# Which products run beside the routing: 96 instead of 76 of 128 expert blocks, at a rate set by how many are left

## The chip, the core and the metric

The kernel runs on one core of one Trainium2 chip. The metric is the device time of one launch in microseconds; lower is better. Engines are named as the profile names them: PE is TensorE (matmuls), PEld its weight loads, DVE is VectorE, ACT is ScalarE, POOL is GpSimd, SP is SyncE, which here only issues DMAs.

## The reference

Two layers of a backbone, each an attention mixer followed by a PEER mixer over 16384 single-neuron experts; 128 prompt tokens and 512 sample tokens. The mixers are not touched. What matters is the second half of each layer:

```python
def peer(h, w_q, sub_keys, u, v):                 # x: tokens x 1024
    q = (x @ w_q).reshape(t, PEER_HEADS, 2, PEER_HALF)
    s = jnp.einsum('thcd,hcnd->thcn', q, sub_keys)
    s1, i1 = lax.top_k(s[:, :, 0], 16)
    s2, i2 = lax.top_k(s[:, :, 1], 16)
    ...                                            # 16 best of the 256 sums
    top_s, pos = lax.top_k(cand, 16)
    idx = jnp.take_along_axis(cidx, pos, axis=-1)
    g = jax.nn.softmax(top_s, axis=-1)
        a = jnp.einsum('td,thkd->thk', xb, u[ib])  # first product
        w = gb * jax.nn.gelu(a)
        return jnp.einsum('thk,thkd->td', w, v[ib])# second product
```

Each token picks 8 x 16 = 128 experts, and their rows of `u` and `v` (1024 floats each) make its output.

## The kernel before

The work is written as Python generators. Each `yield` gives a cost; `weave` runs a main generator and advances side tasks by that cost times their `rate`. What is emitted this way is then ordered on each engine by the scheduler of the framework, and each engine takes its instructions strictly in that order.

For the PEER mixer, 384 of the 512 sample tokens (three tiles of 128) are done densely: all 16384 experts, in 128 blocks of 128 experts, with a gate matrix that is zero where an expert was not picked. The other sample tile and the prompt are done by gathering expert rows with indirect DMAs (`gather_tile`, 256 gathers of 128 rows of 4 KB a tile). Each layer has three stages:

- **Mixer** of the sample, with the prompt's work and gathers beside it.
- **Routing** (`route`, called W in the code): the queries (`peer_q`), the choice of 16 (`pairs`), and then `gate_build` for each of three tiles, which turns indices into dense gate rows on DVE, ACT and PE and writes them to DRAM (`Gd`). A tile has 32 gate steps, each of 4 tokens, 8 small matmuls (L1403, L1404), two evictions (`gst`, L1407) and a `yield 2.2`; three tiles make 96 steps. Beside it runs `dense_pre`: for each block number in `PRE` it loads 512 KB of `ut`, splits it into `uhi` (ACT, L1422) and `ulo` (DVE, L1423), makes the first product for 384 tokens in 24 matmuls (L1434), applies the activation (ACT, tile `gpre`, L1436) and writes 192 KB to DRAM (`Ad`, L1443). What of it is not done when `route` ends is emitted in one piece (`t.drain()`).
- **Dense stage** (`dense`): for each of 128 blocks it loads `v` (512 KB), and either `pre` back from `Ad` (192 KB, blocks in `PRE`) or makes the first product on the spot (`gad`, with its own load of `ut`, for the others); then it multiplies by the gate (`W`, `Whi`, `Wlo`) and adds the second product in 18 matmuls of 512 columns (L1457). The gathers of rows and, in layer 0, the prompt's next mixer run beside it, at rates worked out from the dense stage's total cost.

`PRE` is a rule on the block number: three of every four blocks for the first `Q3` groups of four, two of four for the rest. The rate of `dense_pre` is `AR` = 0.3 up to the end of `peer_q`, `AP_` = 1.75 up to the gate steps, and `AB` = 1.0 in them; a block costs 4.0. The gathers' rate in the dense stage is

```python
total = 4.0 * (256 - len(PRE))
need = 256 * (l + 1)
gath.rate = (need - self.slots) * 3.1 / total * DM
```

so that it follows the dense stage's cost.

Of the kernel before, what the change touches and what calls it, by code (L numbers as in the profile page):

```python
# [28 lines left out]
ND = 384  # L29
NTG = ND // 32  # L30

Q3 = 12
PRE = [i for i in range(128) if i % 4 < (3 if i // 4 < Q3 else 2)]
GBUFS = 8
PTB = 2
# [26 lines left out]
PDR = 0.7  # L62
GA = 0.7
GB = 0.5
AB = 1.0
AR = 0.3
DM = 1.05

# [170 lines left out]
def weave(main, *tasks):  # L239

    tot = 0
    while not main.done:
        cost = main.step()
        tot += cost or 0
        for t in tasks:
            t.advance(cost or 0.0)


class K:
# [1188 lines left out]
    def dense_pre(self, l, Ad):  # L1438
        h = self.ss.h
        for n, i in enumerate(PRE):  # L1440
            ga = self.ph.tile([128, ND], F32, tag="ga", name="gpre", bufs=2)
            self.a_block(l, i, h, n % 8 >= QV, ga)
            self.nc.scalar.dma_start(Ad[n], ga)  # L1443
            yield 4.0

    def dense(self, l, st, h, Gd, Ad, gate):
# [151 lines left out]
    def route(self, l, Gd):  # L1598
        ss = self.ss
        self.ld("iota2", self.nc.scalar, self.ph)  # L1600
        m, gs = self.mg[l]
        ss.h = self.ada(ss, gs[:, 1, :, 1], m[:, 24:32, 1])
        self.flags.add(f"h{l}")
        yield 8.0
        yield from self.peer_q(l, ss)
        self.gath.rate, self.pre.rate = GP, AP_
        yield from self.pairs(ss, 3)
        self.flags.add(f"s{l}")
        yield from self.pairs(ss, 0)
        self.gath.rate, self.pre.rate = GB, AB  # L1610
        n = ND // 128
        for i in range(n):
            build = Task(self, self.gate_build(ss, i, Gd))
            nxt = Task(self, self.pairs(ss, i + 1) if i + 1 < n else iter(()), PRATE)
            build.ctx = nxt.ctx = self.ph, self.wk, self.wb
            while not build.done:
                yield build.step() or 0.0
                nxt.advance(2.2)
            while not nxt.done:
                yield nxt.step() or 0.0  # L1620
# [7 lines left out]
    def run(self, stop=99):  # L1628
# [7 lines left out]
        gath = Task(self, self.gathers(), GRATE)  # L1636
        for l in range(2):
            with self.psum(f"M{l}", mm=2, S=2, tr=1, acc=1):
                sample = Task(self, self.mixer(l, ss))
                if l == 0:  # L1640
                    ma, mp = ExitStack(), ExitStack()
                    pool = ma.enter_context(tc.tile_pool(name="mod1", bufs=1, reuse_waits="tile"))
                    ahead = Task(self, self.mod_strips(1), M1R)
                    ahead.ctx = (pool, pool, 6)
                    pool = mp.enter_context(tc.tile_pool(name="mod0", bufs=1, side="right", reuse_waits="tile"))
                    mod = Task(self, self.mod(0, ("acc", "tr", "acc"), "mw"), 2.0)
                    mod.ctx = (pool, pool, 6)
                    self.constants()
                    old = self.ph, self.wk
                    for st in (ss, sp):  # L1650
                        for _ in range(MS):
                            mod.step()
                        self.ph = self.wk = pool
                        r = self.rstd_x(st)
                        st.r0 = self.cst.tile([128, st.nt], F32, tag="r0" + st.name, name="r0" + st.name, bufs=1)
                        nc.vector.tensor_copy(st.r0, r)
                        self.ph, self.wk = old
                    for _ in range(9 - 2 * MS):
                        mod.step()
                    self.ph = self.wk = pool  # L1660
                    self.decays()
                    self.ld("lam", nc.scalar, pool)
                    self.lam()
                    self.ph, self.wk = old
                    while not mod.done:
                        mod.advance(sample.step())
                    mp.close()
                gath.rate = GRATE if l == 0 else GRATE1
                gath.credit = 0.0
                if l == 0:  # L1670
                    weave(sample, prompt, ahead, gath)
                    ahead.drain()
                    ma.close()
                else:
                    weave(sample, prompt, gath)
                while f"p{l}" not in self.flags:
                    prompt.step()
            gath.rate = GA
            prompt.rate = 0.5
            gath.credit = prompt.credit = 0.0  # L1680
            Gd = self.dram.tile([NTG, 128, 128, 32], F32, name=f"Gd{l}")
            Ad = self.dram.tile([len(PRE), 128, ND], F32, name=f"Ad{l}")
            with self.psum(f"W{l}", mm=W_MM, gb=W_GB), self.sbuf(f"W{l}"):
                ctx = (self.ph, self.wk, 3)
                route = Task(self, self.route(l, Gd))
                pre = Task(self, self.late(f"h{l}", self.dense_pre(l, Ad)), AR)
                self.pre, self.gath = pre, gath
                side = [gath, pre]
                for t in [route] + side[1:]:
                    t.ctx = ctx  # L1690
                weave(route, *side, prompt)
                for t in side[1:]:
                    t.drain()
            with self.psum(f"D{l}", **{f"d{t}{hf}": 1 for t in range(3) for hf in range(2)}, mm=1, pm=1), self.sbuf(f"D{l}"):
                dense = Task(self, self.dense(l, ss, ss.h, Gd, Ad, self.mg[l][0][:, 40:48, 1]))
                dense.ctx = (self.ph, self.wk, 3)
                gath.alias = prompt.alias = "pm"
                self.flags.add(f"d{l}")
                total = 4.0 * (256 - len(PRE))
                gath.credit = prompt.credit = 0.0  # L1700
                prompt.rate = PDR
                need = 256 * (l + 1)
                gath.rate = (need - self.slots) * 3.1 / total * DM
                weave(dense, gath, prompt)
                while f"so{l}" not in self.flags:
                    gath.step()
                while l == 0 and "p1" not in self.flags:
                    prompt.step()
                for t in (gath, prompt):
                    if l:  # L1710
                        t.drain()
                gath.alias = prompt.alias = None
            self.dump(f"xs{l}", ss)
# [39 lines left out]
```

## Time and profile before

| | |
|---|---|
| time, median of 3 runs | 4050.77 us (4027.24 to 4058.07) |
| time of the profiled execution | 4050.72 us |
| its span, first to last instruction | 4048.9 us |
| PE busy / PE weight loads busy | 3653.0 us / 3060.2 us |
| DVE / ACT / POOL busy | 3180.2 us / 1620.7 us / 1621.2 us |
| moved by DMA | 1134.86 MB, mean 280 GB/s |
| gate steps to first dense block, layer 0 / 1 | 1008.3 to 1308.6 us / 2935.3 to 3266.6 us |
| dense stage (first to last `Whi`), layer 0 / 1 | 1308.6 to 2183.2 us / 3266.6 to 4026.2 us |

A busy time is the union of an engine's instructions. Matmuls overlap in the pipeline, so a PE that is busy all the time need not be full; the distance from the start of one matmul to the start of the next tells more. The DMA share is the mean busy share of the 16 DMA engines.

### The profile page before, as it was taken

How to read it: one execution, taken by the hardware profiler on the slowest of the kernel's cores; microseconds unless marked ns; L12 is line 12 of the kernel's file. 1: busy time of each engine (PE TensorE's matmuls, PEld its weight loads, DVE VectorE, ACT ScalarE, POOL GpSimd, SP SyncE). 2: the span in 40 equal slices, each digit the busy share in tenths (PEclk: the TensorE clock that was granted, in tenths of full speed). 3: DMA queues.
4: the chain of work that ended last, by engine and by line, in shares of the span. 5: the costliest groups of instructions: out<-in, count | busy, mean ns of one | idle time of the engine just before them, and what ended most of it. 6: DMA issues, size and time to landing. Idle time of an engine off the chain costs nothing.

```text
span 4048.9 us, 57028 instructions
## 1 busy us (share of the span) xinstructions
PE 3653.0 (90%) x19986; PEld 3060.2 (76%) x19986; DVE 3180.2 (79%) x6370; ACT 1620.7 (40%) x2971; POOL 1621.2 (40%) x1138
## 2 busy tenths in 40 slices
PE   7888889889997999999998898988976999999998
PEld 3675556778886877888886676777875888888887
DVE  3238668999997767778897898899997667777777
ACT  3222223334776433433333333333476634333333
POOL 1004445320554234443464676532075233444342
PEclk9999989999998999999999999999997999999999
DMA  8556778775798889899896777777577889999886
GB/s 320 179 176 235 276 281 281 252 233 181 277 363 323 308 294 358 301 338 347 303 351 250 241 244 231 257 257 232 188 266 274 331 301 333 345 337 324 301 309 213
DMA packets 441087, 1134.86 MB, mean 280 GB/s; under 512 B 40640, under 2 KB 191360, under 8 KB 434528
## 3 DMA queue, kind: packets, MB, share of 16 engines
q0 software_dynamic: 147968, 537.36, 37.7%
q1 hardware_dynamic: 251408, 506.28, 36.3%
q10 hardware_dynamic: 41424, 87.57, 5.8%
q8 instruction: 157, 2.57, 0.2%
q14 instruction: 130, 1.06, 0.1%
HBM read 1045.08 MB, written 85.98 MB: 279 GB/s over the span
## 4 chain that ended last, share of the span: by engine, by line
PE 48%; DVE 16%; DMA 8%; issue 8%; ACT 5%; POOL 2%; ACTq 0%; DVEq 0%; POOLq 0%; SPq 0%
PE d L1457 21%; PE mm L1434 14%; PE mm L478 5%; DMA u<-ut 3%; DVE acc L1340 3%; DVE row L1336 2%; DMA row<-u,xi 2%; PE pm L482 2%; DVE ulo L1423 2%; ACT gst L1407 2%; POOL row L1323 1%; DMA Gd<-gst 1%; ACT uhi L1422 1%; PE S L708 1%; DMA Ad<-gpre 1%
## 5 line engine op out<-in xcount | busy, mean ns | idle before, releaser
L1323 POOL DMA_INDIRECT row<-v,xi x512 | 832.3, 1626 | 1114.1 <-DVE acc L1340 773.6
L1323 POOL DMA_INDIRECT row<-u,xi x512 | 681.3, 1331 | 789.0 <-DVE row L1336 585.2
L1434 PE MATMUL mm<-hhi,uhi 128*128 128x384 f32 x2048 | 709.6, 346 | 46.9 <-ACT uhi L1422 43.2
L1434 PE MATMUL mm<-hhi,ulo 128*128 128x384 f32 x2048 | 707.2, 346 | 49.3 <-DVE ulo L1423 49.1
L1434 PE MATMUL mm<-hlo,uhi 128*128 128x384 f32 x2048 | 702.6, 343 | 2.2 <-DVE hlo L452 1.6
L1336 DVE SCALAR_TENSOR_TENSOR row<-hn,row 128x1024 f32<-128x1024 f32 x512 | 630.0, 1257 | 47.4 <-DMA row<-u,xi 39.8
L1340 DVE SCALAR_TENSOR_TENSOR acc<-row,gw,acc 128x1024 f32<-128x1024 f32 x508 | 650.6, 1281 | 4.2 <-DMA row<-v,xi 1.6
L1457 PE MATMUL d<-vlo,Whi 128*128 128x512 f32 x1536 | 482.1, 394 | 5.6 <-DVE vlo L1498 5.6
L1457 PE MATMUL d<-vhi,Wlo 128*128 128x512 f32 x1536 | 479.0, 393 | 0.0
L1422 ACT CAST uhi<-u 128x1024 fp32r<-128x1024 f32 x256 | 268.8, 1050 | 491.8 <-PE mm L1434 226.8
L1423 DVE TENSOR_TENSOR ulo<-u,uhi 128x1024 fp32r<-128x1024 f32 x256 | 313.5, 1225 | 185.0 <-ACT uhi L1422 183.7
L1457 PE MATMUL d<-vhi,Whi 128*128 128x512 f32 x1536 | 437.3, 397 | 16.9 <-ACT vhi L1497 13.2
L1434 PEld LDWEIGHTS mm<-hhi,uhi 128*128 128x128 f32 x2048 | 396.5, 194 | 65.1 <-ACT uhi L1422 54.4
L1434 PEld LDWEIGHTS mm<-hhi,ulo 128*128 128x128 f32 x2048 | 395.3, 193 | 66.0 <-DVE ulo L1423 62.7
L1434 PEld LDWEIGHTS mm<-hlo,uhi 128*128 128x128 f32 x2048 | 395.2, 193 | 8.7 <-DVE hlo L452 2.0
L1457 PEld LDWEIGHTS d<-vhi,Whi 128*128 128x128 f32 x1536 | 288.1, 190 | 74.9 <-ACT vhi L1497 17.3
L1457 PEld LDWEIGHTS d<-vhi,Wlo 128*128 128x128 f32 x1536 | 288.0, 188 | 61.4 <-issue 0.2
L1457 PEld LDWEIGHTS d<-vlo,Whi 128*128 128x128 f32 x1536 | 286.4, 189 | 62.8 <-DVE vlo L1498 8.0
L1498 DVE TENSOR_TENSOR vlo<-v,vhi 128x1024 fp32r<-128x1024 f32 x256 | 312.2, 1221 | 14.2 <-ACT vhi L1497 13.9
L1505 ACT CAST Whi<-W 128x384 fp32r<-128x384 f32 x256 | 131.2, 513 | 433.1 <-PE d L1457 337.1
L1497 ACT CAST vhi<-v 128x1024 fp32r<-128x1024 f32 x256 | 268.5, 1051 | 53.3 <-DMA v<-v 41.9
L478 PE MATMUL mm<-hhi,whi 128*128 128x512 f32 x624 | 255.4, 410 | 31.5 <-DVE rvs L594 12.6
(470 smaller groups left out, 5776.4 us busy)
## 6 DMA issues: line engine op xcount, KB each, us to landing
u<-ut SPq DMA_DIRECT2D x256, 512.0 KB, 5.3
v<-v SPq DMA_DIRECT2D x256, 512.0 KB, 6.2
Gd<-gst ACTq DMA_DIRECT2D x48, 1024.0 KB, 8.7
G<-Gd SPq DMA_DIRECT2D x64, 768.0 KB, 8.8
w<-win SPq DMA_DIRECT2D x80, 512.0 KB, 4.7
w<-wq SPq DMA_DIRECT2D x64, 512.0 KB, 5.2
Ad<-gpre ACTq DMA_DIRECT2D x152, 192.0 KB, 4.5
pre<-Ad SPq DMA_DIRECT2D x152, 192.0 KB, 6.0
```

What stands on the lines that cost most here:

```text
L478: nc.tensor.matmul(ps[:, :st.T], wp[a][:, k], h[b][:, k], start=(n == 0), stop=(n == 23))
L482: nc.tensor.matmul(ps[:, :st.T], w32[:, k], h[:, k], start=(k == 0), stop=(k == 7))
L1323: nc.gpsimd.indirect_dma_start(out=r, out_offset=None, in_=self.A[f"{'uv'[n // 128]}{l}"], in_offset=bass.IndirectOffsetOnAxis(ap=xi[:, s: ...
L1336: nc.vector.scalar_tensor_tensor(r, hn, 1.0, r, op0=ALU.mult, op1=ALU.mult, accum_out=a[:, s:s + 1])
L1340: nc.vector.scalar_tensor_tensor(acc, r, w[:, s:s + 1], acc, op0=ALU.mult, op1=ALU.add)
L1422: nc.scalar.copy(hi, u)
L1423: nc.vector.tensor_tensor(lo, u, hi, op=ALU.subtract)
L1434: nc.tensor.matmul(ps[:, :ND], u[a][:, k], h[b][:, k, :ND], start=n == 0, stop=n == 23)
L1457: nc.tensor.matmul(acc[t][hf], a[:, ts], b[:, hf * 512:(hf + 1) * 512], start=(i == 0 and n == 0), stop=(i == 127 and n == 2))
L1497: nc.scalar.copy(vhi, v)
L1498: nc.vector.tensor_tensor(vlo, v, vhi, op=ALU.subtract)
L1505: nc.scalar.copy(whi, w)
```

## The change

`Q3` goes from 12 to 32, which is all groups: `PRE` then holds three of every four blocks, 96 instead of 76 of 128. The dense stage makes 32 instead of 52 first products itself, one in every four blocks from start to end. The constant rate `AB` goes; a counter `left`, set to `len(PRE)` and lowered by each block done, gives the rate in the gate steps as the cost of the blocks left over the cost of the 96 steps.

```diff
-Q3 = 12
+Q3 = 32
 PRE = [i for i in range(128) if i % 4 < (3 if i // 4 < Q3 else 2)]
...
-AB = 1.0
...
             self.a_block(l, i, h, n % 8 >= QV, ga)
             self.nc.scalar.dma_start(Ad[n], ga)
+            self.left -= 1
             yield 4.0
...
-        self.gath.rate, self.pre.rate = GB, AB
         n = ND // 128
+
+        self.gath.rate, self.pre.rate = GB, 4.0 * self.left / (n * 32 * 2.2)
         for i in range(n):
...
-                self.pre, self.gath = pre, gath
+                self.pre, self.gath, self.left = pre, gath, len(PRE)
```

Up to some twenty instructions ahead of the first gate step of layer 0 every engine's instructions stand as they did. By the number of `gpre` activations on ACT, the 96 gate steps of layer 0 held 9, 9, 8, 7, 5 and 5 blocks in each sixteenth step before (33 stood ahead of them); now they hold 9, 9, 10, 8, 9 and 14, and 4 more follow. In layer 1 they held 8, 6, 0, 4, 6 and 6, with 35 ahead and 11 behind; now they hold 8, 10, 5, 9, 16 and 13, and none follows.

The first place is ACT at the end of the gate steps of layer 1. `gst` is the eviction of a gate step, `Gd` its write to DRAM, `gpre` a block's activation, `Ad` its write; `uhi` is the next block's split. Before:

```order
L1407 ACTIVATE gst<-gb 128x4x64 x2
L1411 DMA Gd_23104<-gst 128x2048
L1422 CAST uhi<-u_28656 128x1024
L1411 DMA Gd_23104<-gst 128x2048
L1422 CAST uhi<-u_28734 128x1024
L1436 ACTIVATE gpre<-mm 128x384
L1443 DMA Ad_23105<-gpre 128x384
L1436 ACTIVATE gpre<-mm 128x384
L1443 DMA Ad_23105<-gpre 128x384
L1422 CAST uhi<-u_28805 128x1024
L1422 CAST uhi<-u_28853 128x1024
```

Now:

```order
L1406 ACTIVATE gst<-gb 128x4x64 x4
L1442 DMA Ad_23162<-gpre 128x384
L1421 CAST uhi<-u_29981 128x1024
L1435 ACTIVATE gpre<-mm 128x384
L1442 DMA Ad_23162<-gpre 128x384
L1435 ACTIVATE gpre<-mm 128x384
L1406 ACTIVATE gst<-gb 128x4x64 x2
L1442 DMA Ad_23162<-gpre 128x384
L1435 ACTIVATE gpre<-mm 128x384
L1406 ACTIVATE gst<-gb 128x4x64 x2
L1442 DMA Ad_23162<-gpre 128x384
L1410 DMA Gd_23161<-gst 128x2048 x2
```

Before, the last gate writes stand ahead of a tail of blocks; now the last blocks stand between the last gate steps and end with them.

The second place is SP in the dense stage of layer 1, where the blocks used to be half and half: one group of four blocks, from one gate load `G` to the next. `u` is the load for a first product made on the spot, `pre` a reload of one made earlier, `v` the second product's weights. Before:

```order
L1484 DMA G<-Gd_23104 128x12x128
L1467 DMA pre<-Ad_23105 128x384
L1469 DMA v_33102<-v 128x1024
L1416 DMA u_33142<-ut 128x1024
L1469 DMA v_33176<-v 128x1024
L1467 DMA pre<-Ad_23105 128x384
L1469 DMA v_33212<-v 128x1024
L1469 DMA v_33245<-v 128x1024
L1416 DMA u_33284<-ut 128x1024
L1484 DMA G<-Gd_23104 128x12x128
```

Now:

```order
L1484 DMA G<-Gd_23161 128x12x128
L1467 DMA pre<-Ad_23162 128x384
L1415 DMA u_33644<-ut 128x1024
L1467 DMA pre<-Ad_23162 128x384
L1469 DMA v_33678<-v 128x1024
L1467 DMA pre<-Ad_23162 128x384
L1469 DMA v_33719<-v 128x1024
L1469 DMA v_33752<-v 128x1024
L1469 DMA v_33789<-v 128x1024
L1484 DMA G<-Gd_23161 128x12x128
```

One `u` in four blocks gives way to a `pre`; the loads per block grow no fewer.

The third place is DVE at the end of the dense stage of layer 0. `acc<-row` is one gathered row of the fourth sample tile, `xs<-d` and `xs<-pm` add the dense and the gathered result to the stream, and the rows from MEMSET on belong to the next mixer. Before:

```order
L1498 TENSOR_TENSOR vlo<-v_19489,vhi 128x1024
L1501 TENSOR_TENSOR W<-gad,G 128x384
L1506 TENSOR_TENSOR Wlo<-W,Whi 128x384
L1261 SCALAR_TENSOR_TENSOR xs<-pm,mod_121,xs 128x128 x4
L1498 TENSOR_TENSOR vlo<-v_19569,vhi 128x1024
L1261 SCALAR_TENSOR_TENSOR xs<-pm,mod_121,xs 128x128 x4
L1261 SCALAR_TENSOR_TENSOR xs<-d_19626,mod_121,xs 128x128 x4
L1261 SCALAR_TENSOR_TENSOR xs<-d_19635,mod_121,xs 128x128 x4
L1261 SCALAR_TENSOR_TENSOR xs<-d_19647,mod_121,xs 128x128 x4
L1261 SCALAR_TENSOR_TENSOR xs<-d_19656,mod_121,xs 128x128 x4
L1261 SCALAR_TENSOR_TENSOR xs<-d_19668,mod_121,xs 128x128 x4
L1261 SCALAR_TENSOR_TENSOR xs<-d_19677,mod_121,xs 128x128 x4
```

Now:

```order
L1260 SCALAR_TENSOR_TENSOR xs<-d_19713,mod_121,xs 128x128
L1339 SCALAR_TENSOR_TENSOR acc<-row,gw,acc 128x1024
L1260 SCALAR_TENSOR_TENSOR xs<-d_19713,mod_121,xs 128x128 x3
L1260 SCALAR_TENSOR_TENSOR xs<-d_19725,mod_121,xs 128x128 x4
L1260 SCALAR_TENSOR_TENSOR xs<-d_19734,mod_121,xs 128x128 x4
L575 MEMSET kz0s 64x640
L575 MEMSET kz1s 64x640
L1339 SCALAR_TENSOR_TENSOR acc<-row,gw,acc 128x1024
L467 TENSOR_TENSOR wlo<-w_19862,whi 128x1024
L467 TENSOR_TENSOR wlo<-w_19904,whi 128x1024
L1339 SCALAR_TENSOR_TENSOR acc<-row,gw,acc 128x1024 x3
L1260 SCALAR_TENSOR_TENSOR xs<-pm,mod_121,xs 128x128 x8
```

Before, the gather's last row stands ahead of the last block's `W`; now 12 rows follow that `W` (the last five of them are among those shown), and the gathered result is added after the dense one. The number of row operations ahead of the first dense block of layer 0 is 263 in both kernels.

## Rows read from the trace of the kernel before

**Rows 1.** Windows from first gate step to first dense block; each engine's busy us (instructions), clock, DMA.

```profile
1008.30:1118.60 110.30, 101.50 (x718) 95.72 (x717) 106.84 (x145) 78.00 (x173) 63.95 (x21) 0.97 0.79 282
1118.60:1208.20 89.60, 85.29 (x642) 80.18 (x641) 80.32 (x106) 69.59 (x160) 45.76 (x23) 1.00 0.95 355
1208.20:1308.60 100.40, 67.91 (x513) 63.89 (x511) 73.51 (x111) 65.92 (x154) 43.70 (x29) 0.80 0.88 324
2935.30:3030.30 95.00, 76.23 (x586) 70.80 (x585) 95.00 (x127) 68.94 (x155) 74.16 (x13) 0.96 0.76 265
3030.30:3125.00 94.70, 54.65 (x424) 50.59 (x425) 72.61 (x123) 56.26 (x145) 51.78 (x30) 0.73 0.79 289
3125.00:3205.30 80.30, 74.50 (x534) 67.60 (x531) 68.43 (x110) 62.73 (x143) 25.53 (x21) 0.91 0.85 311
3205.30:3266.60 61.30, 51.55 (x282) 49.61 (x282) 21.14 (x26) 21.63 (x37) 5.43 (x5) 0.93 0.68 246
```

**Rows 2.** Such windows, the tile `gpre` alone: ACT's activations, one for each block.

```profile
1008.30:1118.60 110.30, 8.89 (x19) 0.97 0.79 282
1118.60:1208.20 89.60, 7.51 (x15) 1.00 0.95 355
2935.30:3205.30 270.00, 14.68 (x30) 0.87 0.80 287
3205.30:3266.60 61.30, 5.36 (x11) 0.93 0.68 246
```

**Rows 3.** Windows of both dense stages, cut at the 48th block, all engines.

```profile
1308.60:1621.10 312.50, 292.99 (x1491) 251.67 (x1490) 223.06 (x394) 121.94 (x209) 112.67 (x86) 0.97 0.90 321
1621.10:2183.20 562.10, 551.16 (x2852) 487.04 (x2852) 465.75 (x745) 209.77 (x318) 251.26 (x166) 0.99 0.92 328
3266.60:3515.20 248.60, 248.01 (x1169) 212.71 (x1170) 198.82 (x307) 94.91 (x129) 96.78 (x72) 0.99 0.98 344
3515.20:4026.20 511.00, 500.69 (x2387) 438.64 (x2386) 392.47 (x445) 176.79 (x241) 202.24 (x139) 0.99 0.89 308
```

**Rows 4.** The dense stage of layer 1, ACT's `Whi` alone: one for each block.

```profile
3266.60:3515.20 248.60, 24.59 (x48) 0.99 0.98 344
3515.20:4026.20 511.00, 40.98 (x80) 0.99 0.89 308
```

**Rows 5.** Timeline of PE: start us, us, engine, line, operation, tiles, shape, count.

```profile
3206.16 0.33 PE L1434 MATMUL mm<-hhi,uhi 128*128 128x384 f32 x1
...
3215.52 0.33 PE L1434 MATMUL mm<-hhi,uhi 128*128 128x384 f32 x1
...
1151.80 0.22 PE L1403 MATMUL gb<-goi,gjh 128*128 128x128 f16 x1
...
1152.09 0.22 PE L1404 MATMUL gb<-goi,gjl 128*128 128x128 f16 x1
...
3449.65 1.52 PE L1457 MATMUL d<-vhi,Whi 128*128 128x512 f32 x6
...
3457.81 0.84 PE L1457 MATMUL d<-vhi,Whi 128*128 128x512 f32 x3
```

**Rows 6.** The page's groups of instructions: busy us, mean ns of one, idle before it.

```profile
L1340 DVE SCALAR_TENSOR_TENSOR acc<-row,gw,acc 128x1024 f32<-128x1024 f32 x508 | 650.6, 1281 | 4.2 <-DMA row<-v,xi 1.6
...
L1422 ACT CAST uhi<-u 128x1024 fp32r<-128x1024 f32 x256 | 268.8, 1050 | 491.8 <-PE mm L1434 226.8
...
L1423 DVE TENSOR_TENSOR ulo<-u,uhi 128x1024 fp32r<-128x1024 f32 x256 | 313.5, 1225 | 185.0 <-ACT uhi L1422 183.7
```

**Rows 7.** The page's DMA issues: engine, count, KB each, median us to landing.

```profile
u<-ut SPq DMA_DIRECT2D x256, 512.0 KB, 5.3
...
G<-Gd SPq DMA_DIRECT2D x64, 768.0 KB, 8.8
...
pre<-Ad SPq DMA_DIRECT2D x152, 192.0 KB, 6.0
```

**Rows 8.** Window of blocks 33 to 48 of the dense stage of layer 0.

```profile
1494.40:1621.10 126.70, 110.32 (x553) 93.20 (x552) 95.57 (x175) 43.34 (x81) 61.39 (x45) 0.93 0.99 364
```

## The prediction

> **What bounds the kernel now.** I read the windows by stage first, then the spacing of matmuls, since a busy PE says little. In the gate steps the reader is to see three half-full engines rather than one full one [rows 1]: in the first 32 steps of layer 0 DVE is busy for 106.8 of 110.3 us, later it falls to 80.3 of 89.6 and 73.5 of 100.4, and the clock drops with the work: 0.80 at the end of layer 0, 0.73 in the middle of layer 1, so that PE there spends much of its time at 1.2 GHz and is short of work. After the last gate step of layer 1 stand 61.3 us in which DVE is busy for 21.1 us: a tail of first products alone.
>
> In the dense stages PE is the bound, with DMA close behind [rows 3]: layer 1's first 48 blocks have a clock of 0.99, a DMA share of 0.98 and 344 GB/s; its last 80 a share of 0.89.
>
> What PE really needs comes from the spacing [rows 5]. From 3206.16 to 3215.52 lie 54 matmuls of a first product: 0.1733 us each, so a block's 24 cost 4.16 us. From 3449.65 to 3457.81 lie two blocks of second products: 4.08 us a block. Five gate matmuls take 0.29 us, 0.058 each; 32 gate steps have 256 of them, 14.8 us. With 48 and 80 blocks [rows 4], and one first product in four, then two in four, layer 1 needs 48 x 4.08 + 12 x 4.16 = 245.8 us of its 248.6, and 80 x 4.08 + 40 x 4.16 = 492.8 of its 511.0. So the first mix, which the change spreads over all blocks, already runs at PE's pace, but with almost no DMA left over.
>
> **What the change takes from the dense stages.** Each layer loses 20 first products: 20 x 4.16 = 83.2 us of PE; DVE loses 20 x 1.225 us and ACT 20 x 1.05 us and the activations [rows 6], which were not the bound. Layer 1 then needs 128 x 4.08 + 32 x 4.16 = 655.4 us of PE. Its DMAs are the other floor. Busy now: 0.98 x 248.6 + 0.89 x 511.0 = 698 us, for 242.9 MB. Twenty loads of 512 KB become reloads of 192 KB [rows 7]: 6.6 MB less, about 19 us, so 679 us if the engines never rest. The gathers are paced by the stage's cost and are squeezed with it. I take the share that the first 48 blocks kept, 0.98: 679 / 0.98 = 693, a gain of **66 us** of 759.6.
>
> Layer 0 also has the prompt's mixer beside it. Its DMAs are busy for 0.90 x 312.5 + 0.92 x 562.1 = 798 us; less 19, and less 12 rows of 512 KB that the order puts behind the stage (about 18 us), 761. That a full share can starve PE here is seen in blocks 33 to 48: share 0.99, 364 GB/s, and PE busy for only 110.3 of 126.7 us [rows 8]. I take 0.95, between this stage's mean and layer 1's best: 801, a gain of 73. The 12 rows at the end are new: nothing of the next mixer's norm can begin before the gathered tile is added. At 1.28 us a row on DVE [rows 6] that is 15 us, of which the closing matmuls of the last block and the additions hide a few; I charge 12. Layer 0 gains **61 us**. What hides them is that block; without it they cost 15, and more if the rows land late.
>
> The Trainium skill (Perfetto Trace Analysis, Identifying the Most-Contended Engine) says to judge DMA by HBM utilization, because sixteen engines make occupancy misleading, and its Engine Utilization section puts a single active core's ceiling at about 435 GB/s. By that rule layer 1 would need only 236.3 MB / 435 = 543 us of DMA, an estimate, and would stay with PE. This trace so far sides with the share: no window shown passes 364 GB/s.
>
> **What it adds to the gate steps.** Each layer gets the same 83.2 us of PE, 20 x 1.225 us of DVE, 20 x (1.05 + 0.47) us of ACT (the activation is 8.89 us for 19 [rows 2]), 20 issues on ACT's queue for `Ad`, and 20 more loads on SP's queue, where nothing but the loads of the next blocks and of the prompt waits behind them. POOL's queue is passed by nothing: the number of row operations ahead of the dense stage is the same. DVE and ACT have the room: layer 0's three windows sum to 260.7 and 213.5 us, and with 25 and 30 more stay under 290 [rows 1]. The DMAs gain 14.4 MB, of which they can move 355 GB/s at a share of 0.95 [rows 1]: some 40 us, beside the rest. So PE decides, with how well it is fed.
>
> The count of blocks per sixteen steps is known from the order. Layer 0, first 32 steps: 18 blocks before and now, so 110 us as it was; PE needed 19 x 4.16 + 14.8 = 93.8 of 110.3, 0.85. Next 32: 18 instead of 15. Before, 15 x 4.16 + 14.8 = 77.2 of 89.6, 0.86 [rows 1, 2]; now 89.7 / 0.86 = 104. Last 32 with the four that follow: 27 blocks, 127.1 us of PE; DVE has little to add there, so I take 0.90: 141. Sum 355; the blocks at the end cover the last gate writes. From first step to first dense block it was 1008.3 to 1308.6, 300.3 us: a loss of **55 us**.
>
> Layer 1: 18 blocks, 104 as in layer 0 (95.0 before); then 14, whose 73.1 us of PE would fit into the 94.7 us that four blocks took, because something else paced them: 95; then 29, 135.4 / 0.90 = 150. No tail is left to cover the last gate write and the reload of `G` (8.8 us to landing [rows 7]), so I add 12: 361, against 331.3 with the tail. A loss of **30 us**. What pays for the 20 blocks here is the tail of 61.3 us and the starved middle.
>
> **Sum.** The profiled execution took 4050.72 us, its span 4048.9, the median of three 4050.77: no offset. 4050.7 - 66 - 61 + 55 + 30 = 4008.7, **4009 us**.
>
> **Rivals.** *PE alone rules.* If the loads keep up at any share, layer 1's dense stage runs at the 1.011 of its first 48 blocks, 663 us, a gain of 97, and layer 0 gains 83 less 12, 71. If PE is also fed to 0.95 in the crowded steps, layer 0's routing takes 110 + 94 + 134 = 338 and layer 1's 94 + 95 + 142 + 12 = 343, a loss of 50. 4050.7 - 168 + 50 = 3933. For it: in layer 1's first 48 blocks PE was full at a share of 0.98. Against: rows 8. This is also where the page's rule leads; chance 0.20.
>
> *DMA takes the gain back.* The stage's loads wait for few buffers, so the share may stay at the stage's mean instead of rising: 698 / 759.6 = 0.92 in layer 1 and 798 / 874.6 = 0.91 in layer 0. Then layer 1 takes 679 / 0.92 = 738, a gain of 22, layer 0 761 / 0.91 = 836, a gain of 39 less 12, and the routing's 85 us are not paid back: 4050.7 - 49 + 85 = 4087, **slower**. It decides below a share of about 0.94 in both stages. For it: layer 0 has burst at 0.99 beside stretches that average 0.90 [rows 3, 8]. Against: the first 48 blocks of layer 1. Chance 0.15.
>
> *Every block pays what it paid.* In the first 32 steps a block and its share of steps took 110.3 / 19 = 5.8 us. If DVE and ACT's back and forth, not PE, sets that price, layer 0's 63 blocks take 365 and layer 1's 61 take 354 + 12: losses of 65 and 35, 4024 in all. Against it: the later windows, where DVE has room. Chance 0.15.
>
> **How the numbers follow.** About 1%, 40 us, is what a measurement of this kernel can tell from no change: three runs lay 31 us apart. The forecast, 4009, has 0.50, and its own unsure shares (0.95, 0.90) spread it by some 25 us either way, so just over half of it, 0.26, is faster by over 1%, below 4010. With the first rival's 0.20 that is 0.47, rounded; slower by over 1%, above 4091, is the upper part of the DMA rival and a tail, 0.10; the rest, 0.43, lies within 1%. The range reaches half into the fast rival and to just short of the slow one: 3945 to 4070.
>
> **What would show it.** Right: the dense stage of layer 1 near 693 us with a DMA share of 0.97 or more and a PE clock of 0.99; the layer 0 stage near 801 us; the gate steps near 355 and 361 us, with the clock at 0.95 or more in the windows that had 0.80 and 0.73; no stretch of first products alone after layer 1's last step. Wrong: dense stages that end at a share of 0.92 (second rival), or at 663 us (first rival), or gate steps over 375 us with DVE or ACT full; a gap of over 20 us on PE at the end of layer 0's dense stage would mean that the 12 rows cost more than I charge.

## The result and the profile after

Six runs of the changed kernel took 3990.88 to 4011.55 us, median **4001.68**; six of the kernel before 4027.24 to 4065.36, median 4049.47. The ratio is 0.9887, 95% interval 0.9868 to 0.9906: 48 us less, just past the 1% that a measurement of this kernel can tell. The forecast was 4009. The profiled execution took 4011.55 us, the longest of the six, its span 4009.8, against 4050.72 and 4048.9: 39.1 us less. The stages below sum to this second number.

The page of the kernel after: its span, the share of the engines, and the clock in forty slices.

```profile
span 4009.8 us, 57150 instructions
...
PE 3651.4 (91%) x19986; PEld 3045.0 (76%) x19986; DVE 3179.9 (79%) x6370; ACT 1623.5 (40%) x2972; POOL 1615.3 (40%) x1138
...
PEclk9999989999999999999998899989999999999999
```

The windows of the gate steps after, 32 steps a row, layer 0 and then layer 1; the third row of each goes on to the first dense block, and the last two rows cut layer 1's third at its last gate step. They answer to [rows 1].

```profile
1002.10:1105.30 103.20, 97.43 (x710) 91.54 (x709) 101.66 (x138) 76.83 (x168) 81.17 (x13) 1.00 0.77 271
1105.30:1208.90 103.60, 96.39 (x691) 92.22 (x690) 88.88 (x115) 75.36 (x168) 52.51 (x33) 0.95 0.97 367
1208.90:1357.30 148.40, 141.09 (x953) 133.95 (x951) 94.43 (x127) 90.81 (x189) 35.60 (x27) 0.97 0.82 288
2943.40:3051.00 107.60, 96.17 (x693) 90.39 (x692) 103.96 (x140) 75.12 (x166) 57.26 (x20) 0.98 0.81 292
3051.00:3154.40 103.40, 85.39 (x641) 81.98 (x640) 82.45 (x128) 69.51 (x163) 40.95 (x24) 0.92 0.85 307
3154.40:3307.50 153.10, 146.89 (x972) 139.47 (x971) 94.72 (x136) 94.13 (x192) 29.61 (x24) 0.97 0.82 285
3154.40:3292.90 138.50, 137.57 (x928) 131.69 (x927) 90.25 (x130) 86.85 (x176) 29.61 (x24) 1.00 0.80 280
3292.90:3307.50 14.60, 9.32 (x44) 7.78 (x44) 4.48 (x6) 7.28 (x17) 0.00 (x0) 0.77 1.00 335
```

The windows of both dense stages after, cut at the 48th block, as [rows 3]; the last row is blocks 9 to 12 of layer 1.

```profile
1357.30:1669.10 311.80, 288.46 (x1441) 244.16 (x1442) 234.07 (x410) 123.60 (x206) 125.03 (x96) 0.98 0.94 336
1669.10:2171.10 502.00, 477.61 (x2404) 409.37 (x2404) 415.49 (x698) 178.36 (x279) 233.13 (x144) 0.98 0.93 332
3307.50:3570.50 263.00, 252.64 (x1169) 213.97 (x1170) 208.96 (x326) 93.56 (x129) 114.93 (x81) 0.98 0.97 344
3570.50:3987.60 417.10, 411.85 (x1907) 349.73 (x1906) 360.25 (x408) 149.60 (x201) 186.04 (x132) 1.00 0.98 352
3342.80:3374.00 31.20, 25.08 (x97) 19.61 (x96) 18.72 (x28) 7.42 (x11) 11.70 (x9) 0.89 0.88 312
```

The reader is to see the trade. The gate steps, third rows above all, are now full of PE work and the clock is 0.92 to 1.00 where it had been 0.80 and 0.73; they grew from 300.3 and 331.3 us to 355.2 and 364.1. The dense stages shrank, and all of that lies behind the 48th block, where DMA rose from 0.89 to 0.98 in layer 1. The first 48 blocks have as many first products as before and gained nothing: 311.8 us for 312.5, and in layer 1 263.0 for 248.6. Of that loss 10 us lie in blocks 9 to 12, which took 31.2 us instead of 20.8: PE is idle for 6 of them, waiting for the splits of `v`, and its clock is 0.89. Why those came late was not traced. The other kernels with 96 blocks that load everything took 253.7 to 257.2 us for the 48. That is still over 248.6: the gathers' rate rises with a smaller `total`, and where the kernel before ran 72 POOL instructions in these blocks and moved 344 GB/s x 248.6 us = 85.5 MB, the kernel after ran 81 and moved 90.5.

Stage lengths of all kernels, in us: the *gate steps* run from the first `gst` to the first `Whi`, a *dense stage* from its first `Whi` to its last, *between* is from there to layer 1's first `gst`. They are taken from one profiled execution each; the median is over all runs of the kernel.

| kernel | gates 0 | dense 0 | between | gates 1 | dense 1 | span | median (ratio to before, 95%) |
|---|---|---|---|---|---|---|---|
| before | 300.3 | 874.1 | 752.6 | 331.2 | 759.1 | 4048.9 | 4049.47 |
| after | 355.1 | 813.9 | 772.3 | 364.0 | 680.2 | 4009.8 | 4001.68 (0.9868 to 0.9906) |
| e1_rate | 300.8 | 872.1 | 757.8 | 326.0 | 751.4 | 4036.6 | 4041.63 (0.9964 to 0.9999) |
| e2_number | 373.0 | 827.9 | 760.1 | 412.7 | 672.9 | 4075.0 | 4074.44 (1.0037 to 1.0087) |
| e5_86 | 322.5 | 847.9 | 750.3 | 347.7 | 705.5 | 3994.6 | 3994.24 (0.9835 to 0.9900) |
| e4_112 | 407.3 | 786.0 | 756.0 | 409.9 | 663.6 | 4047.1 | 4056.05 (1.0013 to 1.0049) |
| e3_dm | 355.1 | 846.2 | 748.1 | 383.7 | 670.5 | 4022.2 | 4024.47 (0.9914 to 0.9949) |
| e8_91dm | 343.4 | 851.4 | 743.0 | 364.9 | 689.5 | 4016.8 | 4022.95 (0.9914 to 0.9946) |
| e6_reload | 352.1 | 780.0 | 769.4 | 370.2 | 672.6 | 3974.5 | 3972.24 (0.9777 to 0.9823) |
| e7_lean | 342.2 | 833.1 | 758.7 | 348.4 | 672.3 | 3982.1 | 3978.62 (0.9789 to 0.9835) |
| e9_after_ck | 354.1 | 806.0 | 761.5 | 359.6 | 675.2 | 3978.9 | 3975.97 (0.9806 to 0.9849) |
| e10_before_ck | 300.1 | 841.0 | 755.3 | 323.2 | 757.6 | 3999.3 | 4006.15 (0.9878 to 0.9918) |
| e11_86_ck | 316.6 | 826.1 | 761.5 | 352.1 | 705.5 | 3985.4 | 3993.20 (0.9845 to 0.9887) |
| e12_share | 337.5 | 817.6 | 753.9 | 326.3 | 672.9 | 3934.6 | 3940.53 (0.9706 to 0.9774) |

*Between* runs no line of the change but the rows that reach into it, yet spreads from 743 to 772 us; a difference of ten microseconds in one stage of one execution is not read as an effect below unless a row shows its cause.

### The profile page after: what moved, and what is told of

Its sections match the earlier page's. It is cut to its first block, busy times and chain, and to the rows that moved or that the text cites. A ratio compares the mean times of both kernels' runs of the same rounds, so it can differ in the third digit from the quotient of the medians.

```text
span 4009.8 us, 57150 instructions
## 1 busy us (share of the span) xinstructions
PE 3651.4 (91%) x19986; PEld 3045.0 (76%) x19986; DVE 3179.9 (79%) x6370; ACT 1623.5 (40%) x2972; POOL 1615.3 (40%) x1138
## 5 line engine op out<-in xcount | busy, mean ns | idle before, releaser
L1322 POOL DMA_INDIRECT row<-v,xi x512 | 818.4, 1598 | 1097.0 <-DVE acc L1339 753.1
L1322 POOL DMA_INDIRECT row<-u,xi x512 | 690.5, 1349 | 837.3 <-DVE row L1335 599.8
L1433 PE MATMUL mm<-hhi,ulo 128*128 128x384 f32 x2048 | 710.9, 348 | 52.9 <-DVE ulo L1422 52.1
L1433 PE MATMUL mm<-hhi,uhi 128*128 128x384 f32 x2048 | 706.8, 345 | 34.1 <-ACT uhi L1421 32.1
L1433 PE MATMUL mm<-hlo,uhi 128*128 128x384 f32 x2048 | 699.0, 341 | 1.6 <-DVE hlo L451 1.6
L1457 PE MATMUL d<-vlo,Whi 128*128 128x512 f32 x1536 | 486.3, 398 | 20.4 <-DVE vlo L1498 19.9
L1433 PEld LDWEIGHTS mm<-hhi,ulo 128*128 128x128 f32 x2048 | 393.9, 192 | 74.6 <-DVE ulo L1422 72.6
L1433 PEld LDWEIGHTS mm<-hhi,uhi 128*128 128x128 f32 x2048 | 394.7, 193 | 46.7 <-ACT uhi L1421 40.7
L1457 PE MATMUL d<-vhi,Whi 128*128 128x512 f32 x1536 | 406.9, 395 | 25.4 <-ACT vhi L1497 19.9
L1433 PEld LDWEIGHTS mm<-hlo,uhi 128*128 128x128 f32 x2048 | 393.7, 192 | 5.5 <-DVE hlo L451 2.0
```

What stands on the lines that cost most here:

```text
L1322: nc.gpsimd.indirect_dma_start(out=r, out_offset=None, in_=self.A[f"{'uv'[n // 128]}{l}"], in_offset=bass.IndirectOffsetOnAxis(ap=xi[:, s: ...
L1433: nc.tensor.matmul(ps[:, :ND], u[a][:, k], h[b][:, k, :ND], start=n == 0, stop=n == 23)
L1457: nc.tensor.matmul(acc[t][hf], a[:, ts], b[:, hf * 512:(hf + 1) * 512], start=(i == 0 and n == 0), stop=(i == 127 and n == 2))
```

## The experiments

The theory was that of the prediction: the dense stages pay 83.2 us of PE each for twenty blocks fewer until DMA holds them, and the gate steps take the blocks at PE's pace. Against it stood PE alone, DMA alone, and a price of a block that is set by its feeding.

### The two halves of the change: e1_rate and e2_number

The new rate without the new number:

```diff
-Q3 = 32
+Q3 = 12
```

> The new rate alone, with 76 blocks as before. If the gain comes from moving 20 first products into steps where PE is short of work: nothing to gain here, the time is that of the kernel before, 4050 us within 15, and both dense stages stay at 875 and 760 us. If the gain comes from the even deal itself: at least half of it appears, 4025 us or less.

It measured 4041.63 us, ratio 0.9981: at most a few microseconds. All stages are those of before within 8 us.

The new number without the new rate:

```diff
-        self.gath.rate, self.pre.rate = GB, 4.0 * self.left / (n * 32 * 2.2)
+        self.gath.rate, self.pre.rate = GB, 1.0
```

> 96 blocks with the old constant rate 1.0, so that some 20 blocks of each layer stand as a tail behind the gate steps. If what counts is that the added blocks lie beside gate steps: the dense stages are as in the changed kernel (814 and 681 us), but the stretch from first gate step to first dense block grows to some 365 us in layer 0 and 400 in layer 1, and the time is 4030 to 4055 us, no gain left or little. If only the number counts, wherever PE does them: 4002 us within 10.

It measured 4074.44, slower than before. Windows of e2_number from the last gate step to the first dense block, layer 0 and 1:

```profile
1288.30:1379.30 91.00, 86.66 (x494) 85.04 (x493) 26.12 (x26) 32.72 (x52) 0.00 (x0) 0.98 0.57 192
3250.40:3380.00 129.60, 124.86 (x714) 123.23 (x712) 39.82 (x37) 47.11 (x73) 1.88 (x2) 0.99 0.60 199
```

In them stand 19 and 29 blocks (`gpre`) that were left over, near PE's pace: 474 and 694 of the matmuls are theirs (L1433), 474 x 0.1733 = 82.1 us of 91.0 and 694 x 0.1733 = 120.3 of 129.6. DVE and ACT are nearly idle, DMA is at 0.57 and 0.60. The dense stages had their gain (46 and 86 us); the gate steps with these tails took 73 and 82. The time lies above both expected ranges. So neither half does it: the number brings the gain, the rate avoids its price.

### How many: e5_86 and e4_112

```diff
-Q3 = 32
+Q3 = 22
```

> 86 blocks instead of 96, dealt by how many are left. If PE sets the dense stages all the way down: half of the gain, layer 1's dense stage near 715 us, 4025 us within 12. If DMA takes over in the second half of the step: three quarters of the gain or more are there already, 4012 us or less.

With 86 blocks: 3994.24, where 96 had 4001.68 and the two intervals overlap. Half the number gave all of the gain: the dense stages fell by 26 and 54 us for 41.6 us of PE, and the gate steps grew by only 22 and 17. Tails of 10 and 15 blocks stand behind them (none and 11 before); I take it that they cover the last gate writes, which was not tested.

```diff
-PRE = [i for i in range(128) if i % 4 < (3 if i // 4 < Q3 else 2)]
+PRE = [i for i in range(128) if i % 4 < 3 or i % 8 == 3]
```

> 112 blocks, 16 in a layer more than the changed kernel. If DMA is now the floor of the dense stages: layer 1's stops near 655 us (681 with 96) although its PE needs only 589, and each layer's gate steps grow by 60 to 75 us, so 4070 to 4110 us. If PE alone ruled the dense stages: layer 1's falls to 615 us or less, and the time is 4000 to 4020 us.

With 112: 4056.05, no gain over the kernel before. The gate steps took 52 and 46 us more than with 96, less than the 60 to 75 expected; the dense stages returned 28 and 17. Windows of e4_112 in the dense stage of layer 1, cut at the 48th block:

```profile
3358.80:3601.50 242.70, 225.14 (x1025) 185.98 (x1026) 201.46 (x318) 84.31 (x117) 115.07 (x81) 0.99 1.00 361
3601.50:4022.40 420.90, 380.26 (x1667) 308.26 (x1666) 345.98 (x396) 133.23 (x182) 172.94 (x131) 0.99 0.96 342
```

PE needs 128 x 4.08 + 16 x 4.16 = 589 us here and is idle for 58 of the 663.6; DMA is at 1.00 and 0.96. I read this as the DMA floor: (361 x 242.7 + 342 x 420.9) / 1000 = 231.6 MB at a mean of 349 GB/s. Every kernel with 96 blocks ended at 670 to 680 us, just above it, with a PE need of 655.4: there the two floors lie close together.

### What holds the dense stages: e6_reload

One `pre` in four blocks and one `G` in four groups are loaded, and the others use the tile that is there; the products are then those of wrong blocks.

```diff
-                gas[i] = ph.tile([128, ND], F32, tag="pre", name="pre", bufs=4)
-                nc.sync.dma_start(gas[i], Ad[PRE.index(i)])
+                if i % 4 == 0:
+                    self.held = ph.tile([128, ND], F32, tag="pre", name="pre", bufs=4)
+                    nc.sync.dma_start(self.held, Ad[PRE.index(i)])
+                gas[i] = self.held
...
+            if q % 4 == 0:
```

> The changed kernel with less to load in the dense stages: one gate load in four and one reload of first products in three is made and its tile used again, so the result is not the reference's; some 31 MB less a layer, all matmuls kept. If DMA holds the dense stages above PE's pace: layer 1's goes from 680 to 660 to 668 us, which is PE's floor, and layer 0's from 814 to 760 to 790. If PE holds them alone: 680 and 814 within 5.

It measured 3972.24. The windows of e6_reload: the second part of layer 0's dense stage, then both parts of layer 1's:

```profile
1655.40:2140.50 485.10, 476.61 (x2444) 411.03 (x2443) 423.02 (x718) 185.64 (x290) 238.56 (x151) 0.99 0.88 313
3280.10:3532.00 251.90, 248.28 (x1170) 211.99 (x1171) 208.39 (x326) 93.62 (x128) 118.54 (x81) 0.99 0.90 310
3532.00:3952.70 420.70, 412.61 (x1907) 351.33 (x1906) 356.69 (x408) 149.32 (x201) 175.89 (x132) 1.00 0.86 303
```

In layer 1 DMA fell from 0.98 to 0.86, and the 80 blocks took 420.7 us instead of 417.1: PE sets this part, and the full DMA beside it costs nothing. The whole stage, 672.6, lies between the two expected ranges. It is 8 us shorter than after, by its first 48 blocks, and as long as those of e2_number and e7_lean, which load everything. In layer 0 the same bytes were worth 34 us, although the stop on POOL that the next section finds was longer here (88.3 us for 46.6): there DMA held the stage.

### The rows behind the stage: e3_dm and e8_91dm

The price by which the dense task is weighed against the gathers is raised, so that the twelve rows come before the end of layer 0's stage.

```diff
-DM = 1.05
+DM = 1.1
```

> The changed kernel with the gathers of the dense stage paced 1.10 instead of 1.05, so that one gathered row instead of 12 is left behind layer 0's last block. If these 12 rows are a pure loss at the stage's end: the first norm of the next mixer stands 10 us nearer to the last dense block, the dense stage of layer 0 stays at 814 us, and the time falls by 10 to 20 us, to 3990 or less. If DMA is what the stage is short of: the rows' 6 MB go back into it, the stage grows by 10 to 18 us, and the time stays within 8 us of the changed kernel.

> 91 blocks, gathers paced 1.10. With 86 blocks the time was 3994 and with 96 it was 4002, of which 10 to 20 us are the rows behind layer 0's dense stage. If the count has a flat best near 90: 3980 to 3995 us. If the rows' DMA goes back into the dense stage: 3995 to 4005.

(e8_91dm has Q3 = 27 besides, 91 blocks.) They measured 4024.47 and 4022.95, slower than the kernel after. The last `Whi` is followed by the next mixer's first norm after 26.5 and 25.1 us instead of 42.7, as meant; but layer 0's dense stage became 32 and 38 us longer (in e8_91dm five more first products, 20.8 us, are part of that), and layer 1's gate steps 20 in e3_dm, for which no row was found. Neither range of either expectation holds. Windows of blocks 17 to 32 and 33 to 48 of that stage in e3_dm, and of blocks 17 to 32 in the kernel before:

```profile
1451.10:1544.70 93.60, 93.02 (x475) 80.41 (x474) 58.40 (x97) 39.44 (x62) 24.05 (x19) 1.00 0.77 259
1544.70:1672.30 127.60, 110.94 (x556) 93.44 (x554) 105.54 (x197) 43.74 (x82) 72.94 (x54) 0.95 1.02 386
1401.00:1494.40 93.40, 92.97 (x475) 80.53 (x474) 58.05 (x97) 42.22 (x67) 20.03 (x17) 1.00 0.75 250
```

This is the pattern of the kernel before, whose third row here runs up to [rows 8]: a quiet stretch, then a burst in which PE starves. No term of the prediction has a place for it. The waits of POOL in this stage name it; first the kernel before, then after (engine, line, waited for: total us, times, longest):

```profile
POOL ckp L922 <- PE pm L712: 93.8, 2, 78.4
```

```profile
POOL ckp L921 <- DMA pre<-Ad: 46.6, 1, 46.6
```

`ckp` is the clearing of the padded keys of the prompt's next mixer, on POOL's queue like the gathers. Its tile `ck` has two buffers, so the clearing stands until an old one is read, and the gathers stand behind it. (The `pre<-Ad` that the profile names after is its inference from times; that the buffers are what is missing is shown below, where more of them end the wait.) When it goes, the rows that were held up come at once. The stop was 78.4 us before, 46.6 after, 76.9 in e3_dm and 89.3 in e8_91dm: the new price brought it back. Nor does the change itself shorten it: with the same 96 blocks it was 77.4 us in e2_number, e7_lean and e12_share. Of the kernels with two buffers only the one after and e4_112 (49.7) have a short one; what in their order makes it so was not traced.

### The stop taken away: e9_after_ck, e10_before_ck and e11_86_ck

Two buffers more for the prompt, in the kernel after, in the one before, and with 86 blocks:

```diff
-                st.ck = self.ph.tile([128, 2, st.nk], F32, tag="rk" + n, name="ck" + n, bufs=2)
+                st.ck = self.ph.tile([128, 2, st.nk], F32, tag="rk" + n, name="ck" + n, bufs=2 if st.sample else 4)
```

> The changed kernel with four instead of two buffers for the prompt's padded keys (ck) in layer 1's mixer, so that POOL's clearing of one never waits and the gathers behind it on POOL do not stop; the gate steps' order stays block for block, and no gathered row is left behind layer 0's last block. If the stop and the burst of rows after it cost PE time in layer 0's dense stage: the stage falls from 814 to 790 to 805 us, and the time to 3970 to 3985. If only the bytes count there, however they are spread: the stage stays within 6 us, only the rows behind it are saved, and the time is 3990 to 4000.

> The kernel before with the same four buffers. If the stop of POOL (78 us) and the burst cost time: layer 0's dense stage falls from 874 to 845 to 860 us, and the time to 4020 to 4035. If only the bytes count: 874 within 6 and the time 4043 to 4055. Against the run above it gives the change without that stop: 40 to 50 us if the gain is the moved products' own, 20 or less if the shorter stop made most of it.

> 86 blocks and four buffers. 86 blocks gave 3994 us with a stop of 77 us on POOL. If the stop costs what it should in the other two: 3965 to 3980 us. If it costs nothing: 3990 to 4000.

No `ckp` wait is left on POOL in any of the three. The kernel before went to 4006.15 by this alone, some 45 us less; the one after to **3975.97**, 26 us less and the best that computes all of the reference. Windows of e10_before_ck, blocks 17 to 32, 33 to 48 and 1 to 48 of layer 0's dense stage, and of e9_after_ck, blocks 1 to 48:

```profile
1391.50:1485.70 94.20, 93.19 (x474) 80.44 (x473) 75.83 (x131) 41.92 (x66) 39.56 (x30) 1.00 0.98 345
1485.70:1582.40 96.70, 93.44 (x474) 80.46 (x474) 74.63 (x127) 40.53 (x63) 36.91 (x28) 1.00 0.98 346
1298.90:1582.40 283.50, 276.32 (x1412) 238.71 (x1411) 220.10 (x382) 120.55 (x195) 111.97 (x82) 1.00 0.97 344
1354.70:1659.00 304.30, 289.98 (x1476) 248.35 (x1477) 234.32 (x412) 123.10 (x208) 127.83 (x92) 0.98 0.97 347
```

Before, the two took 93.4 and 126.7 us [rows 8]; now 94.2 and 96.7, at an even DMA share. PE is full in both. The stage fell by 33 us, to 841.0, more than expected. In e9_after_ck no row is left behind layer 0's stage, and the norm comes after 29.9 us instead of 42.7; the stage itself fell by only 8 us, to 806.0, just outside both expected ranges, while the time is in the first; the 12 rows are in the stage again. Without the stop on either side, the change is worth 4006.15 - 3975.97 = 30 us by the medians, between the two values that the expectation set against each other. The profiled executions differ by only 20.4: dense stages 35 and 82 less, gate steps 54 and 36 more, the stretch between 6 more.

The rows show what the stop had hidden in layer 0: with it the first 48 blocks took 312.5 us before and 311.8 after; without it 283.5 and 304.3, at a DMA share of 0.97 in both. So the change costs 21 us in these blocks, where it moves no product and the gathers come denser. Behind them it gains 60 us with the stop and 56 without.

With 86 blocks the same edit gave nothing by the medians: 3993.20 against 3994.24. Layer 0's dense stage is 22 us shorter, as it should be without its 77 us stop, but the stretch between is 11 longer and layer 1's gate steps 4; why is open. Without the stop 96 blocks are thus 17 us ahead of 86.

### What a block costs in the gate steps: e7_lean and e12_share

e7_lean does only the first of the three terms in the last twenty blocks of a layer, 8 matmuls instead of 24; e12_share uses the split weights of the block before in three of four blocks behind the 34th, so 47 have no load and no splits.

```diff
+        terms = ((0, 0),) if self.lean else ((0, 0), (0, 1), (1, 0))
...
+            self.lean = n >= 76
```

```diff
-        u = self.u_block(l, i, pre)
+        if not self.share:
+            self.u = self.u_block(l, i, pre)
+        u = self.u
...
+            self.share = n > 33 and n % 4 > 0
```

> The changed kernel with 8 instead of 24 matmuls in each of the last 20 first products of a layer that run beside the gate steps (two of three precision terms left out, so less exact); their loads, splits, activations and writes stay. 55 us of PE less a layer. If PE sets the price of an added block: first gate step to first dense block falls from 355 to 305 to 325 us in layer 0 and from 364 to 320 to 340 in layer 1. If the back and forth of DVE and ACT sets it: both stay within 12 us.

> The changed kernel where beside the gate steps only one block in four loads and splits its weights, and the next three use them again, so the result is not the reference's; all 24 matmuls, activations and writes of each block stay. A block loses 512 KB of load, the split on ACT and on DVE, and keeps its 4.16 us of PE. If PE alone sets the price of a block: the stretch from first gate step to first dense block stays within 10 us of 355 in layer 0 and of 364 in layer 1. If how the blocks are fed (loads, splits, buffers) sets it: 322 to 332 in layer 0, which is PE's need there, and 325 to 340 in layer 1.

Taking 20 x 16 x 0.1733 = 55 us of matmuls out of each layer's last blocks shortened the gate steps by 13 and 16 us: too little for PE alone as the expectation had it, and just over the 12 of the other reading. Some of its blocks fell behind the gate steps: in the window of e7_lean from layer 0's last gate step to the end of its last block, `gpre` alone,

```profile
1288.70:1334.40 45.70, 6.34 (x13) 0.81 0.84 310
```

13 blocks take 3.5 us each, though PE needs 1.4 for one; in layer 1 17 blocks take 3.2 each (3220.5 to 3275.6). Gathered rows run beside them, so loads and splits need 3.5 us at most there, which is less than PE's 4.16. From 4.16 to 3.5 is 13 us for twenty blocks, to 3.2 is 19: about what was gained. Taking most loads and splits away gave 18 and 38. The windows of e12_share from the first gate step to the first dense block:

```profile
1004.80:1342.30 337.50, 324.16 (x2339) 313.45 (x2338) 231.19 (x332) 201.87 (x475) 135.49 (x72) 0.97 0.72 251
2913.80:3240.10 326.30, 317.41 (x2307) 306.52 (x2304) 227.77 (x356) 200.90 (x472) 137.39 (x68) 0.98 0.71 252
```

PE is idle for 13 and 9 us here, after for 20 and 36. The waits of PE in both kernels show the difference; after, layer 0 and layer 1, then the same in e12_share, layer 1:

```profile
PE mm L1433 <- DVE ulo L1422: 7.1, 9, 2.1
PE mm L1433 <- ACT uhi L1421: 7.7, 7, 2.2
PE mm L1433 <- DVE ulo L1422: 6.6, 7, 3.2
PE mm L1435 <- DVE ulo L1422: 0.3, 1, 0.3
```

With ACT's 2.2 in layer 0, PE waited 9 and 14 us for splits after, and for under 1 us in e12_share. For its 63 and 61 blocks (the count in the prediction) PE needs 306 and 298 us by the spacing of its matmuls, not the 322 that the expectation took for layer 0; the rest up to 324 and 317 busy us are other matmuls and stretches that run slower, which were not told apart. So a block's price in the gate steps is PE's in the main, and its feeding adds to it by making PE wait. Neither expectation holds in both layers. What the feeding needs beside the gate steps, where DVE and ACT have more to do than in the lean stretch, stays open; more load buffers, which would have shown it directly, were not tried.

## Why the prediction was right, and where by luck

**Gate steps, 55 and 30.** Measured 54.8 and 32.8. By 32 steps, 110, 104 and 141 stand against 103.2, 103.6 and 148.4; 104, 95 and 162 with the 12 against 107.6, 103.4 and 153.1. The sums hold better than their parts. The clock was to be 0.95 or more in the windows that had 0.80 and 0.73: one shows 0.97; the middle of layer 1 shows 0.92, with PE busy for 85.4 of 103.4 us, so it is still short of work there; what paces it was not traced. What I had too long in layer 1 was the 150, not the 12 for the last reload: the 29 blocks took 138.5 us, with PE fed to 135.4 / 138.5 = 0.98 instead of 0.90, and from the last gate step to the first dense block it was 14.6. No stretch of first products alone is left in layer 1.

**Dense stage of layer 1, 66.** Measured 78.9, and the term that was mis-sized is the 679 us of DMA time. The share came as taken: 0.97 x 263.0 + 0.98 x 417.1 = 664 us busy of 680.2, 0.976. But the 237.3 MB (344 x 263.0 + 352 x 417.1 GB/s us) needed 664 us of it, 357 GB/s while busy, where 242.9 MB had needed 698 us, 348. I had held the rate while busy fixed at the old mean. Nor did DMA alone set the stage: with a share of 0.86 to 0.90 e6_reload still takes 672.6, against PE's need of 655.4.

The Trainium skill (DMA: Bandwidth & Descriptors, Specifications) gives about 358 GB/s as one core's share of the memory, half of what two cores have, below the 435 of the page that the prediction weighed. e4_112 lies near the lower: 361 and 342 GB/s where PE was not the bound. It is no hard ceiling: e3_dm moved 386 over 127.6 us.

**Dense stage of layer 0, 61.** The stage gave 60.2 instead of 73, the share 0.93 instead of 0.95; 0.94 x 311.8 + 0.93 x 502.0 = 760 us of busy time, against the 761 taken. The twelve rows behind it cost 10.4 instead of 12. The end of that stage on DVE in the kernel after:

```profile
2170.45 2.59 DVE L1339 SCALAR_TENSOR_TENSOR acc<-row,gw,acc 128x1024 f32<-128x1024 f32 x2
2174.57 6.56 DVE L1339 SCALAR_TENSOR_TENSOR acc<-row,gw,acc 128x1024 f32<-128x1024 f32 x5
...
2181.04 3.45 DVE L1260 SCALAR_TENSOR_TENSOR xs<-d,mod,xs 128x128 f32<-128x128 f32 x13
...
2193.32 3.91 DVE L1339 SCALAR_TENSOR_TENSOR acc<-row,gw,acc 128x1024 f32<-128x1024 f32 x3
...
2213.88 4.04 DVE L444 SCALAR_TENSOR_TENSOR ada_t<-xs,gs,mm 128x512 f32<-128x512 f32 x6 [1.56 <-PE mm L409]
```

Seven of the twelve rows stand ahead of the additions of the dense result, one among them and four behind, and the norm (`ada_t`) begins 42.7 us behind the last `Whi`, against 32.3. The share and the busy time came near and the cause was only half seen. I read [rows 8] as what a full DMA does to PE; it was the burst after POOL's stop. e9_after_ck and e10_before_ck put the change without the stop at 35 us here, so 25 of the 60 hang on a stop that is 32 us shorter and on the rows left behind; nothing in my sum had the stop, nor the 21 us that the denser gathers cost in the first 48 blocks. How the 25 divide was not measured. With the stretch up to the norm, which pays for the rows, the change is worth 49.8 us with the stops and 39.9 without.

**The sum.** Against the profiled execution before: gates +54.8 and +32.8, dense -60.2 and -78.9, between +19.7, start -6.2, end -1.2: -39.2. The forecast was -42. Layer 0 short by 13 and layer 1 over by 13 cancel; of the 19.7 between the stages the rows explain 10.4. The medians differ by 48.

**The rivals.** *PE alone rules* is nearly so in layer 1's last 80 blocks (its whole stage 680.2, against 663 there and 693 in mine), not in layer 0, where e6_reload bought 34 us with bytes alone, nor in the gate steps. *DMA takes the gain back* is out for 96 blocks: the shares rose to 0.93 and 0.976, and though 0.93 is just under the 0.94 that it set, layer 0's stage took 813.9, not its 836. With 112 the dense stages returned 45 us of 133 that PE had less to do, for 98 in the gate steps: there it is what happened. *Every block pays what it paid* missed in layer 0 (65 against 55); in layer 1 its 35 is as near to the 33 as my 30. Its mechanism is there, but second: feeding takes 3.2 to 3.5 us a block to PE's 4.16, and made PE wait for 9 and 14 us.

## What to carry to other kernels

Work that is moved from a bound stage to a half-empty one pays until the first stage meets its next floor and the second its own pace: measure one step to either side, for here 86 and 96 gave the same (until the stop on POOL was gone) and 112 gave it all back. Move it with its dealing: the same number at a constant rate was slower than not moving it. And when a stretch has a quiet half and a bursting half, look at what stopped an in-order queue ahead of the burst; two buffers were worth as much to the kernel before as the change (45 and 48 us), 26 to the one after, and nothing with 86 blocks. A stop that happens to differ between two kernels can also pass for part of what a change earns: without it the 48 us were 30.

## What the runs showed that was not expected

The DMA share, counted by when packets start, can stand at 1.02 of a window, with 386 GB/s (e3_dm, 127.6 us). At a share of 0.98, two stretches moved 344 GB/s (layer 1's first 48 blocks before) and 352 (its last 80 after), and one of 0.97 moved 367 (the second row of the gate steps after): the share says how busy the engines are, not how much they move. A clearing on POOL stood for 78.4 us in front of gathers that needed nothing from it, and two buffers that end it took 33 us from that stage and some 45 from the kernel before. With 86 blocks a stop of 77.4 us went the same way, and the time did not fall.
